# A norm's factors loaded as 4 KB, turned on TensorE and applied behind the transposes of h

## The chip, the cores and the metric

The kernel runs on one core of one Trainium2 chip. The metric is the device time of one execution in microseconds (us); several executions are timed, and the median counts. PE stands for TensorE, DVE for VectorE, ACT for ScalarE, POOL for GpSimd and SP for SyncE. POOL and SP also issue DMAs: SP's go through the hardware queue q1, POOL's through the software queue q0.

## The reference

Two blocks of two layers each work on 256 rows of 1024 floats. Every sub-layer begins with a norm whose result goes into a matrix product:

```python
def rmsnorm(x, g):
    xf = x.astype(jnp.float32)
    y = xf * lax.rsqrt(jnp.mean(xf * xf, axis=-1, keepdims=True) + EPS)
    return (y * g.astype(jnp.float32)).astype(x.dtype)

# first block: h = x
#   layer 0: retention(rmsnorm(h, norm_mix[0])), dense SwiGLU(rmsnorm(h, norm_ffn[0])),
#            per-layer embedding with sigmoid(rmsnorm(h, norm_ple[0]) @ w_gate)
#   layer 1: band attention with keys and values from rmsnorm(h, norm_kv) and queries
#            from rmsnorm(h, norm_mix[1]); a mixture of 8 experts; the embedding again
#   rmsnorm(h, norm_final)
# second block: twice hybrid mixer(rms_norm(x, norm_mix)), mlp(rms_norm(x, norm_mlp))
```

Everything is float32. Products of matrices are made three times, with each operand split into a high and a low part.

## The kernel before

**Weights.** One stream of about 560 tiles of up to 1 MB is fetched by SP in a fixed order, at most four ahead (more in the expert layer). Each tile is split by ACT (a rounded copy, `whi`, L288) and DVE (the rest, `wlo`, L289), and PE multiplies `whi*xth`, `wlo*xth` and `whi*xtl` (L339 to L341; the order of operands depends on the layer).

**A norm.** `normed_T` makes the transposed, split input of a layer: the residual stream `h` (2 blocks b of 128 rows, 1024 columns, in halves n of 512) times the norm's factors. The factor of a row, `1/rms`, is applied later to the result. `gain_row` loads the 1024 factors into all 128 partitions (512 KB) by a DMA of POOL. For each (b, n) `turned_h` multiplies on DVE (`xs<-h,gain`, L392), turns four 128x128 pieces on PE (`tp<-ident,xs`, L379), and splits what stands in PSUM (`xth` by ACT, L344; `xtl` by DVE, L345). It is called at eleven places: for retention, the dense layer, the two embeddings (`ple`), twice for the band attention (once for keys and values, `xkv`; once for queries, `xq`, put into the program between the halves of the value product), `last_norm`, two mixers, of which the first takes over what `last_norm` made, and two MLPs. The router has a norm of its own, which is not touched.

**The order of the work.** A scheduler puts the instructions of each engine into one fixed order, by a priority that follows the program; each engine then runs its list strictly in order. What stands under `high_priority(offset=300)` is moved forward by 300 places: `turned_h` and the last additions to `h` (`residual`, L471 and L473) are. So the norm of block 0 is made while PE still sums up block 1 (`acc`). `gain_row` and what a function does outside of that `with` keep their place in the program.

**The branch.** Behind the experts a branch on data (L1105) separates the instruction lists: nothing is moved over it by the scheduler except what the program order and the priority already put ahead. Behind it come `last_norm`, with `ple(1)` in it, and then the second block, whose mixer begins with small loads by POOL: `qkn` (the factors of the attention's head norms, in all partitions) and `onorm`.

**Buffers.** All norms' factors are in one buffer of the pool `gains` (one of it), except `gf` and `gm` in `last_norm` and one of the band's. A DMA into that buffer waits until the one before was used. PSUM has eight banks, picked by `banks`.

Of the kernel before, what the change touches and what calls it, by code (L numbers as in the profile page):

```python
# [11 lines left out]
F32 = mybir.dt.float32  # L12
# [3 lines left out]
AF = mybir.ActivationFunctionType  # L16
# [292 lines left out]
class Program:  # L309
# [76 lines left out]
    def turned_h(self, gain, out, by_half=False):  # L386

        with self.banks(tp="0123"), self.tc.high_priority(offset=300):
            for b, n in [(b, n) for n in range(2) for b in range(NB)] if by_half else [(b, n) for b in range(NB) for n in range(2)]:
                sl = slice(n * 512, (n + 1) * 512)  # L390
                xs = self.work.tile([P, 512], F32, name="xs", bufs=3)
                self.nc.vector.tensor_tensor(xs, self.h[:, b, sl], gain[:, sl], op=ALU.mult)  # L392
                self.transposed([a[:, 4 * n:4 * n + 4] for a in out], xs, b, 4)

    def normed_T(self, gain, by_half=False, pool=None):

        xT = self.xT_tiles(pool)
        self.turned_h(gain, xT, by_half)
# [85 lines left out]
    def run(self):  # L484
        nc, io = self.nc, self.io
        with ExitStack() as st, ExitStack() as self.later, \
# [7 lines left out]
            self.w = Stream(self, [(io["w1"], plan_first()), *((io["we"], plan_expert(i)) for i in range(NE)),  # L494
# [8 lines left out]
            self.g0 = self.gains.tile([P, D], F32, name="gain")  # L503
            g = io["norm_mix"]
            for n in range(2):
                sl = slice(n * 512, (n + 1) * 512)
                nc.sync.dma_start(self.h[:, 0, sl], io["x"][0, :P, sl])
                nc.sync.dma_start(self.g0[:, sl], bass.AP(tensor=g.tensor, offset=g.offset + n * 512, ap=[[0, P], [1, 512]]))
                if n == 0:
                    nc.sync.dma_start(self.ident, io["ident"])  # L510
            self.w.fill(1)
# [149 lines left out]
    def ple(self, l, pu, pool=None):  # L661

        nc, io = self.nc, self.io
        xT, r = self.normed_T(self.gain_row(io["norm_ple"][l]), pool=pool)
# [11 lines left out]
    def dense_layer(self):  # L676
        nc, io = self.nc, self.io
        with ExitStack() as dense:
# [3 lines left out]
            xT, r = self.normed_T(self.gain_row(io["norm_ffn"][0]))  # L682
# [95 lines left out]
    def attention_layer(self):  # L778
# [3 lines left out]
        with self.pool("bando", side="right") as outs, ExitStack() as mid, ExitStack() as first:  # L782
            pool = mid.enter_context(self.pool("band", side="right"))
            inp = first.enter_context(self.pool("bandin"))
            gk, gq = self.gain_row(io["norm_kv"]), self.gain_row(io["norm_mix"][1], pool=inp)
# [9 lines left out]
            xkv, r = self.normed_T(gk, by_half=True, pool=inp)  # L795
            with self.banks(mm="45", tp="7", sc="01", pt="26", po="3"):
                v = pool.tile([P, NB, D], F32, name="v")
                for n in range(2):
# [3 lines left out]
                    if n == 0:  # L802
                        self.turned_h(gq, xq)
# [281 lines left out]
    def moe_layer(self):  # L1085
# [19 lines left out]
        with tc.If(most > P):  # L1105
            with self.pool("moe2") as pool, self.pool("raw2", 2) as raw, \
                    self.pool("hl2", 4) as hl, self.banks(acc="67", mm="45", tp="01", ps="23"):
                again = Stream(self, [(io["we"], plan_expert(i)) for i in range(NE)], 2, 4, raw, hl)
# [6 lines left out]
    def last_norm(self):  # L1115
# [3 lines left out]
        with self.pool("last", side="right") as tmp:  # L1119
            gf, gm = (self.gain_row(ap, pool=tmp, name=n) for ap, n in ((io["norm_final"], "gf"), (io["norm_mix_2"][0], "gm")))  # L1120
# [475 lines left out]
```

## Time and profile before

| | |
|---|---|
| three timed executions | 2441.29, 2443.72 (median), 2446.12 us |
| the profiled execution: its own time, its span from the first to the last instruction | 2441.2 us, 2439.4 us |
| mean granted TensorE clock in the span | 0.993 of full speed |
| DMA | 605.72 MB, 248 GB/s in the mean |

How the rows below are read. Times in a row are in us from the start of the span, means of one instruction in ns. "out<-in" names the tiles. In a timeline row the first number is the start, the second the length; "[a <-X]" at the end says that the engine was idle for a us ahead of the instruction, and what it waited for. PE's instructions overlap in part, so that the start of the next counts, not the length. "PEclk" and the number behind the busy times in the rows by stretches is the granted clock of TensorE as a share of its full speed: 1.00 is 2.4 GHz, 0.50 is 1.2 GHz. "x4" is a count of like instructions in a row.

### The profile page before, as it was taken

To read this page: it belongs to the slowest core of one execution; us is meant where nothing else is said; L and a number is where in the kernel's file an instruction comes from. 1 tells how busy PE (TensorE), PEld (TensorE's weight loads), DVE (VectorE), ACT (ScalarE), POOL (GpSimd) and SP (SyncE) were. 2 spreads that over 40 slices of the span, in tenths; PEclk is the share of its full clock that TensorE was granted. 3 is DMA by queue.
4 is the path that set the end of the run, shared out by engine and by line. 5 is a ranking of instruction groups with operands and counts; after the bars stand their busy time and mean duration, and the time that the engine had idled before them with its cause. 6 is when DMAs were issued, how large, how long until landed. Compare 5 with 4: busy or idle time off the path is not lost. (4 is left out here: it accounts for less than half of the span.)

```text
span 2439.4 us, 35652 instructions
## 1 busy us (share of the span) xinstructions
PE 2382.4 (98%) x13032; PEld 1982.4 (81%) x13032; DVE 1893.5 (78%) x3026; ACT 1569.0 (64%) x2609; POOL 61.4 (3%) x105
## 2 busy tenths in 40 slices
PE   8999999999999999999999999899999999999999
PEld 6978998887876787876788876698789989878998
DVE  6756567768999989899999899878776567877655
ACT  6446555657878777778777789645655554575554
POOL 0000000000000000000000000100000000100000
PEclk9999999999999999999999999899999999999999
DMA  7445555566989998999999999534345554434552
GB/s 285 170 170 209 189 190 190 198 236 256 369 324 394 371 362 327 359 357 409 346 371 345 363 349 398 147 134 160 122 169 201 190 172 147 171 108 178 194 190 109
DMA packets 88393, 605.72 MB, mean 248 GB/s; under 512 B 10480, under 2 KB 12144, under 8 KB 17296
## 3 DMA queue, kind: packets, MB, share of 16 engines
q1 hardware_dynamic: 85792, 593.91, 65.2%
q0 software_dynamic: 2416, 9.44, 1.8%
q8 instruction: 104, 1.70, 0.3%
q14 instruction: 81, 0.66, 0.1%
HBM read 602.26 MB, written 1.05 MB: 247 GB/s over the span
## 5 line engine op out<-in xcount | busy, mean ns | idle before, releaser
L289 DVE TENSOR_TENSOR wlo<-wraw,whi 128x512 fp32r<-128x512 f32 (+1 forms) x1656 | 1383.0, 874 | 371.7 <-ACT whi L288 359.4
L288 ACT ACTIVATE whi<-wraw 128x512 fp32r<-128x512 f32 (+1 forms) x1656 | 1203.7, 776 | 443.9 <-PE mm L340 202.0
L339 PE MATMUL mm<-xth,whi 128*128 128x256 f32 x1296 | 364.5, 281 | 0.0
L341 PE MATMUL mm<-xth,wlo 128*128 128x256 f32 x1296 | 363.2, 280 | 1.2 <-DVE wlo L289 1.2
L340 PE MATMUL mm<-xtl,whi 128*128 128x256 f32 x1296 | 364.0, 281 | 0.0
L341 PEld LDWEIGHTS mm<-xth,wlo 128*128 128x128 f32 x1296 | 246.7, 190 | 2.1 <-DVE wlo L289 1.4
L340 PEld LDWEIGHTS mm<-xtl,whi 128*128 128x128 f32 x1296 | 243.4, 188 | 5.3 <-issue 3.8
L339 PEld LDWEIGHTS mm<-xth,whi 128*128 128x128 f32 x1296 | 243.5, 188 | 3.1 <-issue 1.5
L340 PE MATMUL acc<-wlo,hh 128*128 128x512 f32 x624 | 243.8, 391 | 0.0
L341 PE MATMUL acc<-whi,hl 128*128 128x512 f32 x624 | 243.3, 391 | 0.0
L339 PE MATMUL acc<-whi,hh 128*128 128x512 f32 x624 | 232.0, 392 | 1.3 <-ACT hh L344 1.3
L340 PE MATMUL mm<-wlo,xth 128*128 128x512 f32 (+2 forms) x592 | 231.2, 391 | 0.0
L339 PE MATMUL mm<-whi,xth 128*128 128x512 f32 (+2 forms) x592 | 230.6, 390 | 0.3 <-ACT xth L344 0.3
L341 PE MATMUL mm<-whi,xtl 128*128 128x512 f32 (+2 forms) x592 | 230.2, 389 | 0.5 <-DVE xtl L345 0.5
L339 PE MATMUL mm<-whi,xgh 128*128 128x512 f32 x560 | 226.4, 405 | 2.6 <-ACT whi L288 2.6
L340 PE MATMUL mm<-wlo,xgh 128*128 128x512 f32 x560 | 224.3, 401 | 3.0 <-DVE wlo L289 3.0
L341 PE MATMUL mm<-whi,xgl 128*128 128x512 f32 x560 | 222.8, 398 | 0.0
L1003 PE MATMUL mm<-wlo,xgh 128*128 128x512 f32 x336 | 143.3, 426 | 5.4 <-DVE wlo L289 4.6
L339 PEld LDWEIGHTS acc<-whi,hh 128*128 128x128 f32 x624 | 117.4, 188 | 26.5 <-ACT hh L344 3.3
L341 PEld LDWEIGHTS acc<-whi,hl 128*128 128x128 f32 x624 | 117.3, 188 | 25.0 <-DVE hl L345 0.5
L340 PEld LDWEIGHTS acc<-wlo,hh 128*128 128x128 f32 x624 | 117.3, 188 | 23.2 <-DVE wlo L289 0.3
L1002 PE MATMUL mm<-whi,xgh 128*128 128x512 f32 x336 | 134.2, 400 | 0.0
(386 smaller groups left out, 3121.6 us busy)
## 6 DMA issues: line engine op xcount, KB each, us to landing
wraw<-in_we_dram SPq DMA_DIRECT2D x336, 1024.0 KB, 5.8
wraw<-in_w_dram SPq DMA_DIRECT2D x218, 1024.0 KB, 4.8
wraw<-in_w_dram SPq DMA_DIRECT2D x4, 912.0 KB, 4.6
wraw<-in_w_dram SPq DMA_DIRECT2D x6, 512.0 KB, 3.6
bias<-in_rel_rows_dram POOLq DMA_DIRECT2D x4, 768.0 KB, 4.6
gain<-in_norm_ffn_dram POOLq DMA_DIRECT2D x2, 512.0 KB, 6.5
gn<-in_ret_gn_dram SPq DMA_DIRECT2D x4, 256.0 KB, 3.2
gain<-in_norm_ple_dram POOLq DMA_DIRECT2D x2, 512.0 KB, 5.7
```

The costliest lines, as they stand in the source:

```text
L288: self.nc.scalar.activation(h, src, AF.Copy)
L289: self.nc.vector.tensor_tensor(l, src, h.bitcast(F32), op=ALU.subtract)
L339: mm(out, l[0], r[0], start=start, stop=False)
L340: mm(out, l[0], r[1], start=False, stop=False)
L341: mm(out, l[1], r[0], start=False, stop=stop)
L1002: nc.tensor.matmul(out, x[0], wk[0], start=start, stop=False)
L1003: nc.tensor.matmul(out, x[0], wk[1], start=False, stop=stop)
```

## The change

`gain_cols` takes the place of `gain_row` at ten of the norms. It loads the 1024 factors as 8 rows of 128 (4 KB), turns them on PE into a 128x8 tile in PSUM (`gtp`, in bank 3), and copies that to SBUF with ACT (`gcol`): now the factor of a feature stands in the feature's partition. `turned_h` turns `h` itself, and DVE multiplies the turned piece out of PSUM by the factors (`xs<-tp,gcol`); the split then reads `xs` in SBUF. The band's two norms use one set of turned pieces: for each piece two multiplications and two splits follow, and the separate call for `xq` is gone. `last_norm` multiplies two 128x8 tiles in place of two 128x1024 ones, but still loads `gf` as rows. In addition the experts' weights are passed as one flat array that the kernel views by expert.

```diff
+    def gain_cols(self, ap, engine=None):
+        nc = self.nc
+        rows = self.gains.tile([KD, P], F32, name="grow", tag="gain")
+        (engine or nc.gpsimd).dma_start(rows, ap.rearrange("(k p) -> k p", p=P))
+        tp = self.psum.tile([P, 512], F32, name="gtp", tag="bank3", bufs=1)
+        nc.tensor.transpose(tp[:, :KD], rows, self.ident[:KD, :KD])
+        t = self.small.tile([P, KD], F32, name="gcol")
+        nc.scalar.activation(t, tp[:, :KD], AF.Copy)
+        return t
-    def turned_h(self, gain, out, by_half=False):
+    def turned_h(self, pairs, by_half=False):
         with self.banks(tp="0123"), self.tc.high_priority(offset=300):
             for b, n in [(b, n) for n in range(2) for b in range(NB)] if by_half else [(b, n) for b in range(NB) for n in range(2)]:
-                xs = self.work.tile([P, 512], F32, name="xs", bufs=3)
-                self.nc.vector.tensor_tensor(xs, self.h[:, b, sl], gain[:, sl], op=ALU.mult)
-                self.transposed([a[:, 4 * n:4 * n + 4] for a in out], xs, b, 4)
+                tp = self.bank("tp")
+                for k in range(4):
+                    c = n * 512 + k * P
+                    nc.tensor.transpose(tp[:, k * P:(k + 1) * P], self.h[:, b, c:c + P], self.ident)
+                t3 = tp.rearrange("p (k t) -> p k t", t=P)
+                for gain, out in pairs:
+                    xs = self.work.tile([P, 4, P], F32, name="xs", bufs=3)
+                    nc.vector.tensor_tensor(xs, t3, gain[:, 4 * n:4 * n + 4, None].to_broadcast([P, 4, P]), op=ALU.mult)
+                    self.split_psum(*(a[:, 4 * n:4 * n + 4, b * P:(b + 1) * P] for a in out), xs)
...
-            self.g0 = self.gains.tile([P, D], F32, name="gain")
-                nc.sync.dma_start(self.g0[:, sl], bass.AP(tensor=g.tensor, offset=g.offset + n * 512, ap=[[0, P], [1, 512]]))
                 if n == 0:
                     nc.sync.dma_start(self.ident, io["ident"])
+                    self.g0 = self.gain_cols(io["norm_mix"][0], nc.sync)
...
-            gk, gq = self.gain_row(io["norm_kv"]), self.gain_row(io["norm_mix"][1], pool=inp)
+            gk, gq = self.gain_cols(io["norm_kv"]), self.gain_cols(io["norm_mix"][1])
-            xkv, r = self.normed_T(gk, by_half=True, pool=inp)
+            xkv = self.xT_tiles(inp)
+            self.turned_h([(gk, xkv), (gq, xq)], True)
-                    if n == 0:
-                        self.turned_h(gq, xq)
...
-            gf, gm = (self.gain_row(ap, pool=tmp, name=n) for ap, n in ((io["norm_final"], "gf"), (io["norm_mix_2"][0], "gm")))
-            nc.vector.tensor_tensor(gm, gm, gf, op=ALU.mult)
+            gf = self.gain_row(io["norm_final"], pool=tmp, name="gf")
+            gm, gc = self.gain_cols(io["norm_mix_2"][0]), self.gain_cols(io["norm_final"])
+            nc.vector.tensor_tensor(gm, gm, gc, op=ALU.mult)
             self.ple(1, self.pu, tmp)
```

Three places show how the lists of the engines move. Line numbers behind the change are higher by 16 to 19. First DVE, where retention ends and the dense layer's norm is made: `h<-h,acc` are the four additions to the residual stream (b 0 with two halves, then b 1). Before:

```order
L471 TENSOR_TENSOR h<-h,acc 128x512
L392 TENSOR_TENSOR xs<-h,gain 128x512
L471 TENSOR_TENSOR h<-h,acc 128x512
L392 TENSOR_TENSOR xs<-h,gain 128x512
L345 TENSOR_TENSOR xtl<-tp,xth 128x4x128 x2
L289 TENSOR_TENSOR wlo<-wraw,whi 128x512 x3
L471 TENSOR_TENSOR h<-h,acc 128x512
L289 TENSOR_TENSOR wlo<-wraw,whi 128x512
L392 TENSOR_TENSOR xs<-h,gain 128x512
```

And now:

```order
L488 TENSOR_TENSOR h<-h,acc 128x512 x2
L289 TENSOR_TENSOR wlo<-wraw,whi 128x512 x4
L488 TENSOR_TENSOR h<-h,acc 128x512
L289 TENSOR_TENSOR wlo<-wraw,whi 128x512
L488 TENSOR_TENSOR h<-h,acc 128x512
L409 TENSOR_TENSOR xs<-tp,gcol 128x512 x3
L345 TENSOR_TENSOR xtl<-xs,xth 128x4x128 x3
L409 TENSOR_TENSOR xs<-tp,gcol 128x512
```

All multiplications and splits of the norm, those of block 0 too, have moved behind the last addition. The same is found at the first embedding, both MLPs and the second mixer. On PE the reason is seen, at the same place, between retention's last sums (`acc`) and the dense layer's first products (`mm`); now:

```order
L341 MATMUL acc<-whi,gol 128x512
L405 MATMUL tp<-ident,h 128x128 x4
L392 MATMUL gtp<-ident,grow 128x8
L379 MATMUL tp<-ident,pu 128x128 x2
L405 MATMUL tp<-ident,h 128x128 x4
L379 MATMUL tp<-ident,pu 128x128 x2
L339 MATMUL mm<-whi,xth 128x256
```

The turning of the factors, `gtp`, which keeps its place in the program, stands behind all sums; before, `mm` followed straight on `acc`, and the pieces of block 1 were turned between the first products. Last, behind the branch. On PE, before:

```order
L1105 UNCONDITIONAL_BRANCH x2
L379 MATMUL tp<-ident,xs 128x128 x12
L339 MATMUL mm<-whi,xth 128x512
L379 MATMUL tp<-ident,xs 128x128 x4
L340 MATMUL mm<-wlo,xth 128x512
```

and now:

```order
L1123 UNCONDITIONAL_BRANCH x2
L405 MATMUL tp<-ident,h 128x128 x12
L392 MATMUL gtp<-ident,grow 128x8 x3
L405 MATMUL tp<-ident,h 128x128 x4
L339 MATMUL mm<-whi,xth 128x512
L340 MATMUL mm<-wlo,xth 128x512
```

The three `gtp` belong to `norm_mix_2[0]`, `norm_final` and `norm_ple[1]`, in this order, and the embedding's products follow on the third. POOL, which issues their loads, now reads from the end of the experts on (in brackets the semaphores that an instruction waits for):

```order
L390 DMA grow<-in_norm_mix_dram 8x128 [waits DMASW6_49,DVE_49]
L1120 TENSOR_LOAD load [waits DVE_49]
L1123 COMPARE_AND_BRANCH
L1123 UNCONDITIONAL_BRANCH x2
L349 DMA gf<-in_norm_final_dram 128x1024 [waits DVE_49,DMAHW4_49,PE_49,Activation_49]
L390 DMA grow<-in_norm_final_dram 8x128 [waits DMASW1_49,PE_49]
L369 TENSOR_SCALAR ms<-ss 128x1 [waits Activation_49]
...
L1200 DMA onorm<-in_hgrn_onorm_dram 128x64
L390 DMA grow<-in_norm_ple_dram 8x128 [waits DMASW3_49,PE_49]
L390 DMA grow<-in_norm_mlp_dram 8x128 [waits DMASW7_49,PE_49]
```

Before, the load of `norm_ple[1]` stood ahead of the branch, where now that of `norm_mix_2[0]` stands; it has moved behind two others that use the same buffer, and behind `qkn` and `onorm`.

## Rows read from the trace of the kernel before

**Rows 1.** The page: busy time of each engine and share of the span.
```profile
PE 2382.4 (98%) x13032; PEld 1982.4 (81%) x13032; DVE 1893.5 (78%) x3026; ACT 1569.0 (64%) x2609; POOL 61.4 (3%) x105
```

**Rows 2.** By stretches: length, then busy time of each engine, clock, DMA, GB/s.
```profile
100.00:500.00 400.00, 399.32 (x2515) 351.44 (x2513) 260.44 (x468) 220.46 (x435) 20.29 (x39) 1.00 0.53 187
```

**Rows 3.** Timeline of DVE at the dense layer's norm, block 1.
```profile
211.88 0.69 DVE L392 TENSOR_TENSOR xs<-h,gain 128x512 f32<-128x512 f32 x1
212.48 0.68 DVE L471 TENSOR_TENSOR h<-h,acc 128x512 f32<-128x512 f32 x1
```

**Rows 4.** Timeline of PE and ACT there: last sum, first products, one norm piece.
```profile
211.54 0.39 PE L341 MATMUL acc<-whi,gol 128*128 128x512 f32 x1
211.77 0.28 PE L339 MATMUL mm<-whi,xth 128*128 128x256 f32 x1
...
212.01 0.28 PE L341 MATMUL mm<-whi,xtl 128*128 128x256 f32 x1
...
212.62 0.66 PE L379 MATMUL tp<-ident,xs 128*128 128x128 f32 x4
213.03 0.36 PE L340 MATMUL mm<-wlo,xth 128*128 128x256 f32 x1
...
213.48 0.58 ACT L344 ACTIVATE xth<-tp 128x512 fp32r<-128x512 f32 x1
```

**Rows 5.** One line: a product of PSUM with a broadcast operand, on DVE.
```profile
L707 DVE TENSOR_TENSOR gu<-mm,rrow x21: 682/683/685, 227.2 to 393.3; 128x512 f32<-128x512 f32 x21
```

**Rows 6.** Timeline of PE and DVE at the second mixer's start.
```profile
2019.30 0.43 DVE L1434 TENSOR_TENSOR og<-og,onorm 128x256 f32<-128x256 f32 x1 [5.97 <-DMA onorm<-in_hgrn_onorm_dram]
...
2020.38 0.39 PE L341 MATMUL mm<-xth,wlo 128*128 128x256 f32 x1 [1.24 <-DVE wlo L289]
```

**Rows 7.** Timeline at the band's start: its first product, the embedding's last sigmoid.
```profile
427.12 0.47 PE L339 MATMUL mm<-whi,xth 128*128 128x512 f32 x1
...
429.48 0.69 ACT L668 ACTIVATE psg<-mm,r 128x512 f32<-128x512 f32 x1
```

**Rows 8.** Timeline of PE behind the branch.
```profile
1547.83 2.79 PE L379 MATMUL tp<-ident,xs 128*128 128x128 f32 x12 [4.72 <-DVE xs L392]
...
1550.27 0.78 PE L339 MATMUL mm<-whi,xth 128*128 128x512 f32 x1
...
1552.13 0.63 PE L341 MATMUL mm<-whi,xtl 128*128 128x512 f32 x1
```

**Rows 9.** Timeline of POOL behind the branch.
```profile
1549.18 0.91 POOL L1178 DMA_DIRECT2D qkn<-in_qn_dsa_dram  x1
...
1553.52 0.58 POOL L1181 DMA_DIRECT2D onorm<-in_hgrn_onorm_dram  x1
1554.10 0.53 POOL L349 DMA_DIRECT2D gain<-in_norm_mlp_dram  x1
```

**Rows 10.** DMA issues of 1540 to 1575 us: count, KB, us from issue to landing.
```profile
gf<-in_norm_final_dram POOLq DMA_DIRECT2D x1, 512.0 KB, 5.6
...
gain<-in_norm_mlp_dram POOLq DMA_DIRECT2D x1, 512.0 KB, 14.8
...
qkn<-in_qn_dsa_dram POOLq DMA_DIRECT2D x1, 192.0 KB, 13.7
...
onorm<-in_hgrn_onorm_dram POOLq DMA_DIRECT2D x1, 32.0 KB, 12.8
```

**Rows 11.** DMA issues of the whole run: the quickest landing.
```profile
out_dram<-h SPq DMA_DIRECT2D x4, 256.0 KB, 2.0
```

**Rows 12.** By stretches, as rows 2: the start, and two with a lower clock.
```profile
5.00:10.00 5.00, 1.38 (x6) 1.01 (x7) 1.36 (x3) 1.21 (x3) 0.87 (x2) 1.00 0.99 309
...
1536.00:1538.00 2.00, 2.00 (x6) 1.25 (x6) 2.00 (x4) 1.45 (x4) 0.00 (x0) 0.66 0.00 0
1538.00:1540.00 2.00, 2.00 (x6) 1.38 (x6) 1.70 (x4) 1.07 (x3) 0.00 (x0) 0.50 0.86 262
```

**Rows 13.** Timeline of PE ahead of these two: a wait at an expert's end.
```profile
1535.92 0.50 PE L1002 MATMUL acc<-whi,hh 128*128 128x512 f32 x1 [2.99 <-DVE hh L345]
```

More of the change, by code (lines that the diff above doesn't have):

```diff
@@ L485, in run @@
         nc, io = self.nc, self.io
+        self.we = io["we"].rearrange("(e f) -> e f", e=NE)
         with ExitStack() as st, ExitStack() as self.later, \
@@ L493, in run @@
             self.psum = pool("psum", 1, space=PSUM)
-            self.w = Stream(self, [(io["w1"], plan_first()), *((io["we"], plan_expert(i)) for i in range(NE)),
+            self.w = Stream(self, [(io["w1"], plan_first()), *((self.we, plan_expert(i)) for i in range(NE)),
                                    (io["w2"], plan_second())], self.RAW, self.HL,
@@ L663, in ple @@
         nc, io = self.nc, self.io
-        xT, r = self.normed_T(self.gain_row(io["norm_ple"][l]), pool=pool)
+        xT, r = self.normed_T(self.gain_cols(io["norm_ple"][l]), pool=pool)
         def use(b, ps):
@@ L681, in dense_layer @@
             pl = self.ple_rows(0)
-            xT, r = self.normed_T(self.gain_row(io["norm_ffn"][0]))
+            xT, r = self.normed_T(self.gain_cols(io["norm_ffn"][0]))
             with self.banks(acc="4567", mm="012", tp="3"):
@@ L794, in attention_layer @@
             self.pl1 = self.ple_rows(1)
-            xkv, r = self.normed_T(gk, by_half=True, pool=inp)
+            xkv = self.xT_tiles(inp)
+            self.turned_h([(gk, xkv), (gq, xq)], True)
+            r = self.stat.tile([P, NB], F32, name="r")
+            for b in range(NB):
+                self.row_rms(self.h, b, r)
             with self.banks(mm="45", tp="7", sc="01", pt="26", po="3"):
@@ L1107, in moe_layer @@
                     self.pool("hl2", 4) as hl, self.banks(acc="67", mm="45", tp="01", ps="23"):
-                again = Stream(self, [(io["we"], plan_expert(i)) for i in range(NE)], 2, 4, raw, hl)
+                again = Stream(self, [(self.we, plan_expert(i)) for i in range(NE)], 2, 4, raw, hl)
                 nc.vector.tensor_tensor(slot, slot, self.turn[:, None, 1].to_broadcast([P, NB, NE]), op=ALU.subtract)
@@ L1170, in hybrid @@
             if l:
-                self.x2, self.r2 = self.normed_T(self.gain_row(io["norm_mix_2"][l]))
+                self.x2, self.r2 = self.normed_T(self.gain_cols(io["norm_mix_2"][l]))
             xT, r = self.x2, self.r2
@@ L1524, in mlp @@
         with self.pool("mlp", 3) as pool:
-            xT, rms = self.normed_T(self.gain_row(io["norm_mlp_2"][l]))
+            xT, rms = self.normed_T(self.gain_cols(io["norm_mlp_2"][l]))
             r2 = self.stat.tile([P, NB], F32, name="r2")
@@ L1572, in device_inputs @@
     arrays["w1"] = packed(plan_first(), inputs)
-    arrays["we"] = packed(sum((plan_expert(e) for e in range(NE)), []), inputs).reshape(NE, -1)
+    arrays["we"] = packed(sum((plan_expert(e) for e in range(NE)), []), inputs)
     arrays["w2"] = packed(plan_second(), inputs)
```

5 lines of the change are left out of this document (2 added, 3 removed).

## The prediction, made before the changed kernel was run

> **What bounds the kernel.** I read the page first [rows 1]. PE is busy in 98% of the span, DVE in 78%, and the others less. Then I read the stretches [rows 2]: in the dense layers PE is busy in 399.32 of 400 us at the full clock, with DMA at 0.53 and DVE at 0.65 of the time. So outside of the experts every us in which PE stands still is a us of the result, and what DVE, ACT or DMA save is worth nothing by itself. The next view is the timeline where one layer passes to the next. At the dense layer's norm [rows 3, 4] the reader is to see that nothing is lost there: the last sum of retention starts at 211.54, the first product of the dense layer at 211.77. Block 0's norm was made under the sums of block 1, and block 1's is made under the products of block 0. The change has to be judged by what it does to these seams, and by the one behind the branch, where no cover exists.
>
> **The arithmetic itself is even.** A multiplication takes 0.69 us before, from SBUF [rows 3]. One that reads PSUM with a broadcast operand takes 0.683 us [rows 5], which is the new one's form. The splits stay as many (for the band, too: two sets of four pieces before, four pieces with two sets of splits after). So DVE and ACT have the same to do, and I cost this at nothing. PE saves the band's second set of transposes: four groups, each of which takes 0.41 us out of the products' line (212.62 to 213.03) [rows 4]; this is 1.6 us, and counted in the band's term.
>
> **The seams.** Every `xs` now needs `gcol`, `gcol` needs `gtp`, and the order of PE puts `gtp` behind the last sum of the layer before. So all four multiplications wait for the end of the sums, where two or three were done by then. At the dense layer the last sum ends at 211.93 (211.54 and 0.39). PE turns one piece of block 1 (0.41) and then the factors: about 212.4. The copy by ACT is 8 columns wide; I take 0.3 us with the passing of signals, less than the 0.58 of a full `xth` [rows 4] and not less than zero. Three `xs` follow at 0.60 us each (211.88 to 212.48 [rows 3]) and end at 213.4, 214.0 and 214.6. The first `xth` (0.58) lets the first product go at about 214.1. The third product needs `xtl`, which stands behind the third `xs` on DVE and takes what an addition of that size takes, 0.68 [rows 3]: 215.4. Before, the third product started at 212.01 [rows 4], so it is 3.4 us later. In return two groups of transposes no longer lie between the products: 0.8 us. The seam costs 2.6 us; I take 2.5. The bounds are 1.5 (only the first product is late, 214.1 against 211.77, less 0.8) and 3.5 (nothing is given back). Behind the waiting multiplications on DVE stand the `wlo` of the next weights, but some tiles are split ahead, so I add nothing for them.
>
> The same order stands at the first embedding, the two MLPs and the second mixer. Four seams of 2.5 make 10. At the second mixer PE stood still for 1.24 us shortly afterwards [rows 6], since DVE was held by the landing of `onorm`; that landing doesn't move, so it takes up 1.24 of the 2.5: 1.3 us. The sum is **+11.3** (from 6.5 to 17).
>
> **The band.** Before, its first product started at 427.12 while ACT was still 2.36 us behind with the embedding's last sigmoid, at 429.48 [rows 7]; three pieces of the norm had been prepared by then. Now the copy for `norm_kv` stands behind that sigmoid: 429.48 and 0.69 make 430.2, with 0.3 for the copy, 0.69 for `xs` and 0.58 for `xth` 431.8, and with two splits of weights ahead of `xth` on ACT up to 1 us more. I take 432.1: 5.0 us later. PE gives back four groups of transposes, 1.6 us. DVE then has eight multiplications and eight splits to do, 16 times 0.6 or 9.6 us, of which before a part was done; I add 0.1. The factors for `xq` may only be loaded when those for `xkv` have left the buffer, and the second `gtp` stands two places behind the first product; that load has some 4 us, and needs from 2.0 us (the quickest landing [rows 11]) to 5.6 us (`gf` [rows 10]). **+3.5**, with bounds of 1.5 and 7.
>
> **Behind the branch.** This is the largest term. Before, PE's twelve transposes started at 1547.83, its first product at 1550.27, the third at 1552.13 [rows 8]; the embedding's factors had been loaded long ahead. Now three loads of factors share one buffer, and only the first is ahead of the branch. PE turns twelve pieces (now free from about 1547.0, some 2.6 us), and the first `gtp` at about 1549.6. The second load is issued by POOL at about 1550, behind `gf`, and lands between 1552 (2.0 us [rows 11]) and 1555.6 (`gf`'s 5.6 us [rows 10]). The third, `norm_ple[1]`, stands behind `qkn` and `onorm` on POOL. `onorm` was issued at 1553.52 and the load behind it at 1554.10 [rows 9]; POOL is now some 0.7 us later: 1554.8. What a load at that place waits for is seen before: `qkn` landed after 13.7 us, `onorm` after 12.8, so at 1566.3, and the 512 KB behind them after 14.8 [rows 10], of which their own transfer took at most the 3.6 by which `gf` exceeds the quickest landing. So 11.2 us or more of it were a wait in the queue, and a load of 4 KB issued at 1554.8 lands at about 1566. By the Trainium skill ("DMA: Bandwidth & Descriptors", section on queues, rings and completion order) each DMA engine consumes the descriptors of a ring in ring order. By that rule, 4 KB don't pass what was issued ahead of them; the three landings agree.
>
> PE has nothing else in line until then: all products of the embedding stand behind the third `gtp`. From there on it is as at a seam, 3.0 to 3.4 us to the third product: 1569.2 in place of 1552.13, **+17**. The clock is no difference: the first products were at the lower clock before, too (0.78 and 0.63 us for what takes 0.39 elsewhere [rows 4, 8]). Bounds: 14 (landing with `qkn`, at 1562.9) and 20 (landing with what was 14.8 us, at 1569). `last_norm`'s own norm keeps its chain: multiplication and transposes only change places. I cost it at nothing.
>
> **The start.** Two loads of 256 KB leave the queue ahead of the first weights. At the 309 GB/s of that stretch [rows 12] they are 1.7 us; the new steps may eat 0.3 of it. **-1.4**, with bounds of -1.7 and 0, if the first product comes to wait for the factors in place of the weights. The other 4.6 MB that are no longer loaded save nothing: PE is the bound there. The view of the experts' weights as one array changes no address, so nothing.
>
> **The sum.** +11.3 +3.5 +17 -1.4 = 30.4 us. The profiled execution took 2441.2 us, which would be 2471.6; the median of the runs is 2443.72, 2.5 us above it, so the runs should be at 2474.
>
> **The rivals.**
>
> *The last load doesn't queue.* It lands 2.0 us after its issue, at 1556.8 in place of 1566, if its eight rows go to DMA engines that are done with `qkn`. That takes 9.2 us off: 2465. For it: 4 KB are little. Against it: the three landings of more than 12 us [rows 10]. The Trainium skill has a price that speaks for it ("DMA: Bandwidth & Descriptors", section on the anatomy of a DMA by the gpsimd path): about 2.0 us and the bytes at 436 GB/s, in which a queue isn't counted. By that price the load lands 2.0 us after its issue and the time is this rival's; rows 10 disagree with it for this place.
>
> *The clock falls at the seams.* A wait of 2.99 us at an expert's end [rows 13] was followed by two stretches of 2 us at 0.66 and 0.50 of the clock [rows 12], together a loss of 0.68 and 1.0 us. The seams' waits are shorter, and broken by transposes. If it happened at all four seams and in the band, 8.4 us would come on top: 2482.
>
> *The seams are hidden.* DVE and ACT have slack, and PE's waits might be made up where it waits for weights otherwise. Then the branch and the start remain: +15.6, 2459. Against it: PE waits for next to nothing in these layers [rows 2].
>
> *The other side: faster.* Transposes straight from `h` needn't wait for DVE. If all `gcol` were ready in time, PE would begin 0.8 us earlier behind the branch (1547.0 against 1547.83), save 1.6 in the band and 1.4 at the start: 3.8 us less, 2440. It decides itself by whether each `gtp` runs before the last sum starts, and whether the third load lands before 1549.6. The order of PE and POOL speaks against both.
>
> **How the numbers follow.** My forecast has 0.72, the load that doesn't queue 0.11, the clock 0.08, hidden seams 0.05, faster 0.04. The forecast's own range, with its bounds not all on one side, is 2468 to 2480. The range takes in the first two rivals, so 2462 to 2483. A measurement of this kernel can tell about 0.2%, 4.9 us, from no change. Slower by more holds in all cases but the last, and faster by 3.8 us would be within 0.2%; mishaps in my reading of the order are put to both sides: slower 0.94, same 0.03, faster 0.03.
>
> **What the profile would show.** Behind the branch: one wait of PE of some 14 to 17 us for the DMA of `norm_ple`, and POOL's issue of it at about 1554 or 1555 us. At each seam: PE idle for 2 to 3 us, for `xth` and then `xtl`; at the band 4 to 5 us. At the start: the first product 1 to 1.7 us earlier. PE's busy time lower by 1 to 2 us. What would make this wrong: a landing of the last load within 3 us of its issue; a `gtp` that runs before the sums end; or PE filled during the waits by work that I have not seen.

## The result: slower by 21 us, and the profile after

Six runs of each: 2465.72 us in the median with the change (2462.36 to 2467.42), 2444.47 before; the ratio is 1.0086, with an interval from 1.0073 to 1.0099. The profiled execution spans 2460.6 us, 21.2 more than before, where the prediction's sum was +30.4. Two views show most of it. The page, as [rows 1]: PE has the same work, and it is the idle time that grew (2460.6 less 2383.1, or 77.5, against 2439.4 less 2382.4, or 57.0).

```profile
PE 2383.1 (97%) x13027; PEld 1974.2 (80%) x13027; DVE 1890.2 (77%) x3026; ACT 1571.9 (64%) x2620; POOL 55.8 (2%) x106
```

The waits of PE (what waited, for what: us in total, times, longest). Two are new and long, both a `gtp` that waits for its load; of the seven short ones for `xth`, one lies at each norm that waits for its factors: dense layer, both embeddings, band, second mixer and both MLPs.

```profile
PE gtp L392 <- DMA grow<-in_norm_ple_dram: 7.2, 1, 7.2
PE gtp L392 <- DMA grow<-in_norm_final_dram: 6.8, 1, 6.8
PE mm L339 <- ACT xth L344: 5.2, 7, 1.2
```

The timeline of the dense layer's norm, which answers to [rows 3, 4]. The reader is to follow one chain: last sum at 210.85, `gtp`, `gcol`, three multiplications, `xth`, and the first product at 214.12, that is 3.27 us behind the start of the last sum, where before it came 0.23 us behind it. On ACT, `gcol` and `xth` each start where a sum of squares of `h` (`junk`) ends.

```profile
210.85 0.40 PE L341 MATMUL acc<-whi,gol 128*128 128x512 f32 x1
...
211.65 0.61 ACT L367 ACTIVATE junk<-h 128x512 bf16<-128x512 f32 x1
...
211.70 0.22 PE L392 MATMUL gtp<-ident,grow 8*128 8x8 f32 x1
...
212.26 0.15 ACT L394 ACTIVATE gcol<-gtp 128x8 f32<-128x8 f32 x1
...
212.46 1.88 DVE L409 TENSOR_TENSOR xs<-tp,gcol 128x512 f32<-128x512 f32 x3
...
212.84 0.62 ACT L367 ACTIVATE junk<-h 128x512 bf16<-128x512 f32 x1
...
213.45 1.14 ACT L344 ACTIVATE xth<-xs 128x512 fp32r<-128x512 f32 x2
...
214.12 0.38 PE L339 MATMUL mm<-whi,xth 128*128 128x256 f32 x1 [0.58 <-ACT xth L344]
...
215.02 0.38 PE L341 MATMUL mm<-whi,xtl 128*128 128x256 f32 x1 [0.40 <-DVE xtl L345]
```

The stretches around it, as [rows 2] (busy PE, PEld, DVE, ACT, POOL, then the clock). Behind the 0.86 us and then 0.52 us in which PE stood still, the granted clock is at 0.50, that is 1.2 GHz, for 216 to 218. The same is seen at the first MLP's seam (0.50 in 1844 to 1846).

```profile
212.00:214.00 2.00, 1.14 (x8) 0.69 (x7) 2.00 (x4) 2.00 (x8) 0.30 (x1) 1.00 0.92 319
214.00:216.00 2.00, 1.48 (x8) 1.28 (x9) 1.90 (x4) 2.00 (x6) 1.85 (x4) 0.89 0.36 149
216.00:218.00 2.00, 2.00 (x12) 2.00 (x11) 2.00 (x4) 0.80 (x2) 0.55 (x2) 0.50 0.62 179
```

The timeline of PE and POOL behind the branch, which answers to [rows 8, 9]. Each load is issued only when the `gtp` before it has freed the buffer (1551.96 and 1552.53; 1559.04 and 1559.57), and the second and third `gtp` wait for theirs.

```profile
1551.96 0.27 PE L392 MATMUL gtp<-ident,grow 8*128 8x8 f32 x1
...
1552.53 0.52 POOL L390 DMA_DIRECT2D grow<-in_norm_final_dram  x1 [2.22 <-PE gtp L392]
...
1553.49 0.92 POOL L1197 DMA_DIRECT2D qkn<-in_qn_dsa_dram  x1
...
1556.66 0.58 POOL L1200 DMA_DIRECT2D onorm<-in_hgrn_onorm_dram  x1
...
1559.04 0.24 PE L392 MATMUL gtp<-ident,grow 8*128 8x8 f32 x1 [6.80 <-DMA grow<-in_norm_final_dram]
...
1559.57 0.54 POOL L390 DMA_DIRECT2D grow<-in_norm_ple_dram  x1 [2.34 <-PE gtp L392]
1566.48 0.24 PE L392 MATMUL gtp<-ident,grow 8*128 8x8 f32 x1 [7.21 <-DMA grow<-in_norm_ple_dram]
...
1568.38 0.79 PE L339 MATMUL mm<-whi,xth 128*128 128x512 f32 x1 [0.27 <-ACT xth L344]
```

The DMA issues there, as [rows 10] (KB, us to landing). The same 4 KB take 6.4 and 6.8 us behind `gf` and `qkn`, and 2.2 when the queue is empty again. The load for the embedding lands at 1566.4, just behind `onorm` (1556.66 and 9.5, or 1566.2), which was issued ahead of it.

```profile
qkn<-in_qn_dsa_dram POOLq DMA_DIRECT2D x1, 192.0 KB, 12.4
...
onorm<-in_hgrn_onorm_dram POOLq DMA_DIRECT2D x1, 32.0 KB, 9.5
grow<-in_norm_final_dram POOLq DMA_DIRECT2D x1, 4.0 KB, 6.4
grow<-in_norm_ple_dram POOLq DMA_DIRECT2D x1, 4.0 KB, 6.8
grow<-in_norm_mlp_dram POOLq DMA_DIRECT2D x1, 4.0 KB, 2.2
```

Where the 21 us arise is read by the starts of the same products in two timelines. The table gives the start before, and by how much the same product starts later (+) or earlier in the changed kernel and in two of the experiments below.

| product | before, us | changed | x10 | x9 |
|---|---|---|---|---|
| retention, behind its first weights | 20.11 | -1.55 | -1.91 | -1.85 |
| retention's last sum | 211.54 | -0.69 | -1.59 | -0.97 |
| dense layer's first sum | 241.94 | +2.60 | +0.16 | -0.97 |
| dense layer's last sum | 404.44 | +0.22 | +0.14 | -3.42 |
| first embedding, near its end | 427.12 | +2.91 | +4.24 | -3.51 |
| band, in its projections | 454.13 | +4.36 | +5.98 | -5.49 |
| experts' end | 1541.65 | +2.17 | +7.69 | -8.82 |
| first mixer's start | 1582.06 | +16.48 | +23.34 | -11.22 |
| first mixer's last sum | 1824.80 | +15.62 | +23.09 | -11.92 |
| first MLP's first sum | 1838.06 | +19.64 | +27.65 | -11.87 |
| first MLP's last sum | 2005.06 | +18.89 | +27.79 | -12.26 |
| second mixer, behind its start | 2020.61 | +20.41 | +30.41 | -11.38 |
| second mixer's last sum | 2254.94 | +19.72 | +30.61 | -9.91 |
| second MLP's first sum | 2269.05 | +21.85 | +34.03 | -10.73 |
| second MLP, near its end | 2433.93 | +21.10 | +34.03 | -11.48 |

All columns are single executions, so a difference of about 1 us in one place proves little: x6 to x8 below, which leave the start alone, are +1.4, -0.5 and +0.1 us in the first row. The differences from row to row are the terms. The places that the change touches: start -1.55, dense seam +3.29, first embedding +2.69, band +1.45, branch +14.31, first MLP +4.02, second mixer +1.52, second MLP +2.13; together **+27.9**. And the bodies of the layers, in which nothing was to change: +0.86 in retention, -2.38 in the dense layer, -2.19 in band and experts, -0.86, -0.75, -0.69 and -0.75 in the last four; together **-6.8**. No step of the prediction has these. In band and experts x10 has +1.7 and x9 -3.3, so the -2.19 there needn't all be one thing; the dense layer's -2.38 is -0.02 in x10 and -2.45 in x9.

### The profile page after: what moved, and what is told of

The parts are those of the page before. It is cut to its first block, busy times and chain, and to the rows that moved or that the text cites. A ratio compares the mean times of both kernels' runs of the same rounds, so it can differ in the third digit from the quotient of the medians.

```text
span 2460.6 us, 35656 instructions
## 1 busy us (share of the span) xinstructions
PE 2383.1 (97%) x13027; PEld 1974.2 (80%) x13027; DVE 1890.2 (77%) x3026; ACT 1571.9 (64%) x2620; POOL 55.8 (2%) x106
## 5 line engine op out<-in xcount | busy, mean ns | idle before, releaser
L339 PE MATMUL mm<-whi,xgh 128*128 128x512 f32 x560 | 224.3, 401 | 2.7 <-ACT whi L288 2.6
L339 PEld LDWEIGHTS acc<-whi,hh 128*128 128x128 f32 x624 | 117.5, 188 | 27.9 <-ACT hh L344 3.2
L341 PEld LDWEIGHTS acc<-whi,hl 128*128 128x128 f32 x624 | 117.5, 188 | 27.7 <-DVE hl L345 0.5
L339 PEld LDWEIGHTS mm<-whi,xth 128*128 128x128 f32 x592 | 113.8, 192 | 30.6 <-ACT xth L344 7.5
```

The costliest lines, as they stand in the source:

```text
L339: mm(out, l[0], r[0], start=start, stop=False)
L341: mm(out, l[1], r[0], start=False, stop=stop)
```

## The experiments

The theory after the result: late factors cost the 27.9, in the way that was forecast, and something else makes the products themselves quicker. The rivals: it is the multiplications behind the transposes that cost, or other loads that would be waited for anyway; and the forecast was too high by itself. Each experiment is compared with runs of the kernel before that were made beside it, whose median is given. The edits are shown in part; "..." marks what is left out.

**x1: the three factors behind the branch prepared ahead of it.**

```diff
@@ attention_layer, behind ple_rows(1)
+            rows3 = self.gains.tile([3 * KD, P], F32, name="grow", tag="gain")
+            for i, ap in enumerate((io["norm_mix_2"][0], io["norm_ple"][1], io["norm_final"])):
+                nc.gpsimd.dma_start(rows3[i * KD:(i + 1) * KD], ap.rearrange("(k p) -> k p", p=P))
@@ attention_layer, behind the values: one gtp of 24 rows, gcol3 by ACT, the product gm by DVE
@@ last_norm
-            gm, gc = self.gain_cols(io["norm_mix_2"][0]), self.gain_cols(io["norm_final"])
-            nc.vector.tensor_tensor(gm, gm, gc, op=ALU.mult)
+            gm = self.g3[:, 0]
...
```

> Only the three tiles of factors behind the branch are different from the changed kernel: their rows are loaded during the band attention and turned there, so that behind the branch no load of factors and no gtp is left. Theory (the wait for the loads is the price behind the branch): the first products follow the twelve transposes as before, the time falls by what the two traces differ by there, about 14.5 us, from 2465.7 to about 2451. Rival (the loads only hide another wait, that for the weights or for gf, of the same length): less than 5 us are won, above 2460.

Not shown: the embedding takes `self.g3[:, 1]`, and `gcol` has two buffers in place of four, so that with `gcol3` the tiles keep their places.

Measured: 2447.87 us against 2442.73 (ratio 1.0022, 1.0012 to 1.0033; the ten runs lie between 2444.2 and 2452.4), so 5.1 us above before, where the change was 21.2 above: 16 us of the loss are the loads behind the branch, a little more than the 14.5 expected. The timeline of PE there: sixteen transposes in a row, and the first product behind them without a wait.

```profile
1550.34 3.64 PE L405 MATMUL tp<-ident,h 128*128 128x128 f32 x16 [3.77 <-DVEq L1131]
1553.63 0.77 PE L339 MATMUL mm<-whi,xth 128*128 128x512 f32 x1
```

From the experts' end to the first mixer this kernel is 2.35 us quicker than before (+3.45 and +1.10 by the same products). With the factors there, the new norm is the better one at this place; the rival that hid another wait is out.

**x2a, x2b, x2c: three loads in buffers of their own, at three places of POOL's queue.** `gain_cols` is cut in two here and in x4: `load_cols` takes the tile and issues the DMA, `turn_cols` has `gtp` and the copy. x2a issues them right behind `gf`, x2b ahead of `gf`, x2c has loads like those of `qkn` and `onorm` ahead of the third.

```diff
@@ last_norm, x2a (x2b: the three load_cols stand ahead of gf)
             gf = self.gain_row(io["norm_final"], pool=tmp, name="gf")
-            gm, gc = self.gain_cols(io["norm_mix_2"][0]), self.gain_cols(io["norm_final"])
+            gm, gc = (self.turn_cols(self.load_cols(ap, pool=tmp, name=n)) for ap, n in
+                      ((io["norm_mix_2"][0], "grow1"), (io["norm_final"], "grow2")))
+            self.gple = self.load_cols(io["norm_ple"][1], pool=tmp, name="grow3")
...
@@ x2c, ahead of the last line
+            dq = tmp.tile([P, 8, 64], F32, name="dq")
+            for i, (a, m) in enumerate(((io["qn_dsa_2"][0], 6), (io["kn_dsa_2"][0], 1), (io["hgrn_onorm_2"][0], 1))):
+                j = (0, 6, 7)[i]
+                nc.gpsimd.dma_start(dq[:, j:j + m], bass.AP(tensor=a.tensor, offset=a.offset, ap=[[0, P], [0, m], [1, 64]]))
```

> The changed kernel with a buffer for each of the three tiles of factors behind the branch, so that POOL issues all three right behind gf and none waits for the one before to be turned. Theory (a queue is served in the order of issue): the rows wait until the 512 KB of gf have left the queue, land some 8 to 9 us after their issue, at about 1558, and the first product starts at about 1560 in place of 1568.4: about 8 us won, 2457 to 2458. Rival (4 KB pass what is ahead of them, only the shared buffer cost time): they land 2.2 us after their issue, at about 1553.5, the first product starts at about 1555.5, 13 us won, 2453.

> As x2a_own_buffers, but POOL issues the three loads of 4 KB ahead of gf. Theory (order of the queue): nothing is ahead of them, they land 2 to 2.5 us after their issue, the last at about 1553.5, the first product starts at about 1555.5: 13 us won against the changed kernel, 2453, and 4 to 5 us less than x2a_own_buffers. Rival (4 KB pass what is ahead of them): no difference to x2a_own_buffers by more than 1 us.

> As x2a_own_buffers, but with loads like those of qkn and onorm (256 KB in 256-byte pieces, into a tile that nobody reads) ahead of the load for norm_ple[1]: this is the place that the prediction gave it, without the wait for a buffer. Theory (the queue is in order): issued at about 1555, it lands 11 us later or more, at 1565 to 1567, as late as in the changed kernel, where it was issued at 1559.57. Rival (the wait for the buffer made it late): it lands 2 to 5 us after its issue, before 1560.

Measured: x2a 2457.06 and x2b 2455.35 against 2442.73; x2c, one execution, 2469.04. The DMA issues of x2a, for the loads of `norm_final` and `norm_ple[1]`, both behind `gf`:

```profile
grow<-in_norm_final_dram POOLq DMA_DIRECT2D x1, 4.0 KB, 4.8
grow<-in_norm_ple_dram POOLq DMA_DIRECT2D x1, 4.0 KB, 4.7
```

Those of x2b, ahead of `gf`:

```profile
grow<-in_norm_final_dram POOLq DMA_DIRECT2D x1, 4.0 KB, 2.7
grow<-in_norm_ple_dram POOLq DMA_DIRECT2D x1, 4.0 KB, 2.6
```

And those of x2c, where only the second of the two is behind the 256 KB in small pieces:

```profile
grow<-in_norm_final_dram POOLq DMA_DIRECT2D x1, 4.0 KB, 4.7
grow<-in_norm_ple_dram POOLq DMA_DIRECT2D x1, 4.0 KB, 15.7
```

So the same 4 KB take 2.6, 4.7 or 15.7 us by what was issued ahead of them: they don't pass it. The Trainium skill ("DMA: Bandwidth & Descriptors", section on queues, rings and completion order) says, where it describes the loads of SP and ACT, that each DMA engine takes descriptors in ring order; these rows show the same of POOL's queue. The price of the Trainium skill (same page, section on the anatomy of a DMA by the gpsimd path: about 2.0 us and the bytes at 436 GB/s, so 2.0 us for 4 KB) is near the 2.2 us of the empty queue, and below all the others.

x2a's time came out as expected, but its rows landed 4.7 to 5.1 us after their issue, not 8 to 9. x2b was 1.7 us better than x2a by the medians of four runs each, whose intervals overlap (1.0028 to 1.0061 and 1.0040 to 1.0073), and 2.9 by the traces (experts' end to first mixer: +2.9 against +5.7), less than the 4 to 5 expected: in x2b the twelve transposes end at 1554.58, the first `gtp` follows at 1555.13 and waits for its load for 0.54 only, so an earlier landing had little left to give; from there to the first product, at 1558.10, the three `gtp` with their copies, `xs` and `xth` take 3 us. x2c gives the forecast its answer: at the place that the prediction gave this load (issued at 1552.85 in x2c), and with no buffer to wait for, it lands at 1568.6. That is later than the changed kernel's 1566.4, in which it was issued 6.7 us later.

**x4: the factors of five seams turned one layer earlier.**

```diff
@@ e.g. retention: the load behind its own norm, the gtp behind its values
+        rows = self.load_cols(io["norm_ffn"][0])
...
+            self.gnext = self.turn_cols(rows)
@@ dense_layer
-            xT, r = self.normed_T(self.gain_cols(io["norm_ffn"][0]))
+            xT, r = self.normed_T(self.gnext)
```

> The changed kernel with the factors of five norms (dense layer, first embedding, second mixer, both MLPs) loaded and turned one layer earlier, so that at these seams gcol is there before the last sums end. Band and branch stay as changed. Theory: the five seams cost 3.3, 2.8, 1.6, 3.7 and 2.0 us by the two traces, 13.4 in all, and the order of the list is their cause: 2452 to 2453; PE's clock doesn't fall at 215.6 and 1843.7 any more. Rival (the multiplications behind the transposes, not the late factors, hold the seams): less than 5 us are won, above 2460.

Measured: 2452.36 against 2442.73 (1.0043, 1.0028 to 1.0057), 9.6 above before, 11.6 less than the change's 21.2: as expected. Between them x1 and x4 win 27.7 us; the table has 14.31 and 13.65 at the places that they mend. At the dense layer the product for `xth` starts 0.58 us behind the last sum, with one group of transposes between, and the one for `xtl` has nothing to wait for.

```profile
212.60 0.39 PE L341 MATMUL acc<-whi,gol 128*128 128x512 f32 x1
212.83 0.60 PE L410 MATMUL tp<-ident,h 128*128 128x128 f32 x4
213.18 0.37 PE L339 MATMUL mm<-whi,xth 128*128 128x256 f32 x1
...
213.50 0.28 PE L341 MATMUL mm<-whi,xtl 128*128 128x256 f32 x1
```

The granted clock stays at 1.00 from 211 to 219, and doesn't fall at the first MLP either. It was the late factors, not the order of transposes and multiplications.

**x5: all factors but the first norm's prepared far ahead.** Seven norms' rows are loaded at the start into one tile and turned by one `gtp` in retention, three more during the experts.

```diff
@@ run
+            self.rows = self.load_all((io["norm_ffn"][0], io["norm_ple"][0], io["norm_kv"], io["norm_mix"][1],
+                                       io["norm_ple"][1], io["norm_final"], io["norm_mix_2"][0]))
+            self.gall = self.small.tile([P, 7, KD], F32, name="gall", bufs=1)
...
```

> The changed kernel with all factors but the first norm's prepared far ahead: seven norms' rows in one tile at the start and three in another in the experts' layer, each turned by one gtp. No load, gtp or gcol is left at a seam, in the band's start or behind the branch. Theory (late factors are the whole loss, and the products themselves run quicker by where the tiles lie): the first product of each layer starts as in the kernel before or earlier, 1.8 us are won at the start and 1.6 in the band; with the tiles' places the products take 5 to 10 us less: 2431 to 2438, faster than both. Rival (transposes from h and multiplications behind them cost as such): 2445 or more.

Measured: 2438.16 against 2443.22 (0.9974, 0.9962 to 0.9985). Faster than both kernels, at the upper edge of what was expected: 5.1 us, by its trace from the start, the band and the branch, and nothing from quicker products. In the dense layer their step (the time from the start of one product to that of the next) is that of before. Here `gall` and the first norm's factors take 256 bytes of a partition, in the changed kernel the four buffers of `gcol` take 128 (8 columns of 4 bytes each).

**x6, x7, x8: the kernel before, with tiles at other places only.** x6 has 128 unused bytes ahead of most tiles, x7 opens `bank3` first, x8 does both.

```diff
@@ run, x6
+            pad = self.small.tile([P, KD], F32, name="gcol")
+            nc.vector.memset(pad, 0.0)
@@ run, x7
+            first = self.psum.tile([P, 512], F32, name="gtp", tag="bank3", bufs=1)
+            nc.vector.memset(first[:, :KD], 0.0)
```

> The kernel before, with nothing changed but 128 unused bytes per partition ahead of most tiles in SBUF, which is how far gcol shifts them in the changed kernel. Theory A (the place in SBUF sets the products' step): the sums acc of the dense layers take 232 in place of 227 ns a product and the experts' first products 257 in place of 259, as in the changed kernel; mm with 256 columns stays at 117.5; the whole becomes 3 to 5 us slower, 2446 to 2448. Theory B (PSUM banks): no change, within 1 us of before.

> The kernel before, with nothing changed but the PSUM tag bank3 opened first (a memset of 8 columns at the start), so that the tags bank0 to bank3 lie in banks 1, 2, 3, 0 as in the changed kernel. Theory B (the bank sets the step of mm): mm with 256 columns in the dense layer and the MLPs takes 113.5 in place of 117.5 ns, 3.8, 2.9 and 3.1 us in the three layers, 2433 to 2434 in all. Theory A (SBUF alone): no change, within 1 us of before.

> The kernel before with both, the 128 bytes and the banks' order, so that every tile lies where it does in the changed kernel, with none of its new work. If places alone make the bodies of the layers quicker, this shows the changed kernel's sum over bodies: 5.6 us less than before, 2437 to 2438. If the new norm's work does it, no change.

Measured, against 2443.22: x6 **2435.51** (0.9965, 0.9953 to 0.9977), x7 2443.51 (0.9999, 0.9990 to 1.0008), x8 2434.30 (0.9961, 0.9947 to 0.9975). Both my theories had it wrong: the banks do nothing, and the 128 bytes make the kernel not 3 to 5 us slower but 7.7 faster. x8, expected to be 5.6 us faster than before, is 8.9 faster, without any of the new norm's work. One line of the profile by its duration in the dense layer (min, median, max in ns) shows why; `mm` is the products of 256 columns, `acc` the sums of 512. Before:

```profile
L340 PE MATMUL mm<-xtl,whi x319: 276/281/285, 231.5 to 392.4; 128*128 128x256 f32 x160
L340 PE MATMUL acc<-wlo,hh x80: 389/389/395, 242.2 to 397.7; 128*128 128x512 f32 x80
```

x6:

```profile
L340 PE MATMUL mm<-xtl,whi x319: 276/276/279, 233.7 to 392.1; 128*128 128x256 f32 x160
L340 PE MATMUL acc<-wlo,hh x77: 390/393/404, 244.4 to 395.4; 128*128 128x512 f32 x77
```

The durations overlap, but they differ by what the steps from start to start differ by: `mm` 5 ns less, `acc` 4 ns more. There are four times as many `mm`. The changed kernel has 276 and 393 at the same place, so the bytes of `gcol` are enough to make its bodies quicker; nothing that the norm does is needed for it.

**x9: all factors early and the tiles where the changed kernel has them.** As x5, but at most four norms' factors at a time, in 128 bytes: four are loaded at the start, three in the band (two of them multiplied at once), three during the experts.

```diff
@@ run, against x5
-            self.gall = self.small.tile([P, 7, KD], F32, name="gall", bufs=1)
+            self.gall = self.small.tile([P, 4, KD], F32, name="gall", bufs=1)
...
```

> All factors prepared ahead as in x5_all_early, but at most four norms' at a time in 128 bytes, so that every tile lies where it does in the changed kernel. Theory (late factors and the tiles' places are independent of each other): the 5 us that x5_all_early won and the 7 to 8 that x6_pad won against the kernel before add up: 2430 to 2432, 12 us less than before. Rival (they share one cause): 2435 to 2438.

Measured: **2430.60** against 2443.30 (0.9948, 0.9934 to 0.9961), 12.7 us faster than before and some 34 faster than the change. The 5.1 of x5 and the 7.7 of x6 add up.

**x10: the changed kernel with the tiles where before had them.** Another 128 bytes, 256 in all.

```diff
+            pad = self.small.tile([P, KD], F32, name="pad")
+            nc.vector.memset(pad, 0.0)
```

> The changed kernel with 128 unused bytes more, so that the tiles lie as in the kernel before, modulo 256 bytes. Theory (the forecast's own terms came out near 28 us, and the tiles' places gave 7 back): dense layer and MLPs run at the step of before (117.5 and 227 ns), and the whole is 7 us slower than the changed kernel, 28 us slower than before: 2471 to 2473. Rival (the forecast was too high by itself): no change against the changed kernel, 2464 to 2467.

Measured: **2472.95** against 2443.30 (1.0120, 1.0105 to 1.0136), 29.7 us above before. The dense layer's line is again that of before:

```profile
L340 PE MATMUL mm<-xtl,whi x320: 276/281/281, 231.3 to 392.6; 128*128 128x256 f32 x160
L340 PE MATMUL acc<-wlo,hh x81: 389/389/478, 242.3 to 399.0; 128*128 128x512 f32 x81
```

This is the forecast's own question, asked without the places: +30.4 was forecast, +29.7 measured. That it fits so well is partly luck. In its trace, the slowest of its four runs and 34 us above before, the four seams cost 13.8 us (10 forecast), the second mixer 2.6 (1.3), the band 1.7 (3.5) and the branch 15.7 (17).

**x11: which tiles.** The kernel before, with 128 unused bytes inside three layers' own pools, so that in the dense layer only `hh` and `hl` move, in the first MLP only `r` and `r0`, in the second MLP all.

> The kernel before with 128 unused bytes in three layers' own pools: in the dense layer only hh and hl are moved by 128 bytes, in the first MLP only r and r0 (which ACT and DVE alone touch), in the second MLP all of them. If the place of the operands that PE reads sets the step: mm takes 113.5 in place of 117.5 ns (and acc 232 in place of 227) in the dense layer and the second MLP, and stays in the first MLP. If the accesses of ACT and DVE beside it set it: the first MLP changes and the dense layer doesn't.

One execution: 2440.63. The same line in the dense layer, the first MLP and the second MLP:

```profile
L340 PE MATMUL mm<-xtl,whi x319: 276/276/279, 231.7 to 390.1; 128*128 128x256 f32 x160
L340 PE MATMUL acc<-wlo,hh x80: 390/393/404, 242.4 to 395.5; 128*128 128x512 f32 x80
...
L340 PE MATMUL mm<-xtl,whi x238: 276/281/367, 1832.8 to 1992.9; 128*128 128x256 f32 x119
L340 PE MATMUL acc<-wlo,hh x119: 389/389/395, 1838.0 to 1997.7; 128*128 128x512 f32 x119
...
L340 PE MATMUL mm<-xtl,whi x228: 276/276/367, 2264.0 to 2419.7; 128*128 128x256 f32 x114
L340 PE MATMUL acc<-wlo,hh x112: 390/393/404, 2269.2 to 2417.4; 128*128 128x512 f32 x112
```

It is the place of `hh` and `hl`, the operands of the sums; moving `r` and `r0` does nothing (ACT and DVE alone touch them, but for `r0`, which PE turns at the layer's start). ACT and DVE write `hh` and `hl`, too, so whether PE's reads or these writes do it was not told apart.

## Why the prediction was right, and where it wasn't

The direction and the range held. The point lay 8 us above the result. In the traces, where +30.4 was forecast and +21.1 is found in the last row, 6.8 us of the miss lie outside of the prediction's terms and 2.5 in them. **The step that failed is "the arithmetic itself is even"**, with its "I cost this at nothing". For DVE and ACT it holds (1893.5 and 1890.2 us busy, 1569.0 and 1571.9). But it counted instructions and took each of PE's products as fixed in its duration, and so the prediction has no term for the layers' bodies. The new tile `gcol` moved `hh` and `hl` by 128 bytes, and the products' steps with them: 6.8 us off in the bodies by the traces, 7.7 and 8.4 by the runs (x6 against before, x10 against the change). That the terms miss by 2.5 only is partly luck, since their errors cancel: band and branch were put 4.7 us too high, seams and second mixer 2.4 too low. By its own terms:

- **The seams** (2.5 each): 3.29, 2.69, 4.02 and 2.13. The chain is as described, but a little too short. That the first product was forecast at 214.1 and seen at 214.12 is luck: retention's last sum starts 0.69 us earlier than before. Counted from its start, the first product was forecast 2.56 us later and came after 3.27; the third, forecast after 3.9, came after 4.17. A part of what was missed is ACT's sums of squares, behind which `gcol` and `xth` stand. Then the clock: its fall at a seam had been a rival with 0.08, and came true at two of four. What it costs is seen in x1, x2a to x2c and x10, whose lists at these seams are the same, while the clock fell at other ones. The same products give (us later than before):

| seam | where the clock didn't fall | where it fell |
|---|---|---|
| dense layer | 1.73 to 1.75 (x2a, x2b, x2c, x10) | 3.29 (changed), 3.26 (x1) |
| first embedding | 2.68 to 2.70 (changed, x1, x2a, x2b, x2c) | 4.10 (x10) |
| first MLP | 2.99 (x1) | 4.02 (changed), 4.16 to 4.56 (x2a, x2b, x2c, x10) |
| second MLP | 2.13 (changed), 2.12 (x1) | 3.37 to 3.65 (x2a, x2b, x2c, x10) |

Without a fall the four seams are 9.6 us, against 10 forecast; a fall adds 1.0 to 1.6. The clock is seen in the stretches, as above: at the dense seam of x1, at that of x2a, and at the first embedding of x10.

```profile
217.00:219.00 2.00, 2.00 (x11) 2.00 (x11) 2.00 (x4) 0.93 (x3) 0.65 (x3) 0.50 0.52 123
...
218.00:220.00 2.00, 2.00 (x19) 2.00 (x19) 2.00 (x4) 0.94 (x3) 0.67 (x3) 1.00 0.58 112
...
408.00:410.00 2.00, 2.00 (x6) 1.48 (x7) 1.88 (x4) 1.37 (x3) 0.34 (x1) 0.57 0.00 0
```

- **The second mixer** (1.3): 1.52. The wait at `wlo` behind `onorm`, 1.24 us before, is gone, as forecast. (The bounds of the seams with it, by the prediction's own figures, are 6.3 and 16.3, not 6.5 and 17.)
- **The band** (3.5): 1.45. A row was misread. The product at 427.12 in [rows 7] is still one of the embedding's, behind a piece of the norm; the band's own first product started at 429.28, where the embedding's last sigmoid starts as well (429.48). With that, the forecast's 432.1 is 2.8 us later, not 5.0, and the term becomes 1.3. The band's first product before, and in the changed kernel:

```profile
429.28 0.39 PE L339 MATMUL mm<-whi,xth 128*128 128x512 f32 x1
...
434.66 0.50 PE L339 MATMUL mm<-whi,xth 128*128 128x512 f32 x1 [1.24 <-ACT xth L344]
```

- **Behind the branch** (17): 16.0 at the first product that needs `xtl` (1570.25 less the 2.17 by which the experts end later, against 1552.13), of which 14.31 are left at the first mixer's start; part of the difference is that two more products stand ahead of it now. In place of one wait of 14 to 17 us there are two, of 6.80 and 7.21. The landing was forecast for 1566 and seen at 1566.4, but that fits by luck: with the 2.17 taken off it is 1564.2, and it came about by another way. The step that was left out is the wait for the shared buffer. The load ahead of this one was issued at 1552.53 (1550.4 with the delay taken off, as forecast), and took 6.4 us behind `gf`, not 2.0 to 5.6. So this one was issued at 1559.57, not at 1554.8. From there it took 6.8, not 11.2, since what stood ahead of it had been under way for longer. x2c shows that an earlier issue would not have helped, and x2a and x2b that the place in the queue does.
- **The start** (-1.4): -1.55.

**The rivals.** "The last load doesn't queue" would have given 2465, which is what was measured, and yet it is wrong: the load did queue, here until `onorm` had landed, and in x2c for 15.7 us. A number that fits is no proof of its mechanism. "The seams are hidden" falls with x4. "Faster" was put at 2440 if every factor were ready in time; x5, which makes them ready, gives 2438, and its condition (each `gtp` ahead of the last sums, no load behind the branch) was the right one.

## What to carry to other kernels

A small operand that everything behind it waits for has to be prepared where the scheduler can't sort it behind the work that it serves: its load and its turning belong a layer ahead, in a buffer of its own, and ahead of bulky or finely cut loads in the same queue. The same idea that lost 21 us then wins 5. And before a few us are put down to an edit, the kernel before should be run once with its tiles moved by the bytes that the edit adds: here that alone was worth 8 us.

## What the runs showed of the hardware

The step of TensorE's products depends on where in SBUF the operands of other products lie. With `hh` and `hl` moved by 128 bytes, `acc` takes 393 in place of 389 ns by its rows, and `mm` 276 in place of 281, although the operands of `mm` itself stayed where they were (x11); 256 bytes (x5, x10) are as 0. The 276 is not out of reach before: it is the minimum in its row there. By the starts in the timeline of before, the dense layer's `mm` comes every 118 ns up to 225, every 113 from 231.5, behind products for the embedding, to the first `acc` at 241.9, and every 118 from there on; in x11 it is much the same up to the first `acc`, and then goes on at 113. So the same kind of product, with its own operands at the same place, runs at either step, and the step changes where something else has run in between. Why, stays open. PSUM banks in another order (x7) changed nothing that could be measured.

The granted clock fell to 1.2 GHz at two seams of the changed kernel, behind waits of PE that come in pieces (0.86 us of idle time in 212 to 214, 0.52 in 214 to 216). But whether it falls isn't settled by such a wait: at the dense seam it fell in x1, behind 0.72 us of idle time in 213 to 215 and 0.62 in 215 to 217, and not in x2a, with 0.71 in 214 to 216 and 0.64 in 216 to 218, the same list and the tiles at the same places. Which seams are hit could not have been read from the trace of before.
